# Grouped instance norm on one core: 64 KB rows in every unit but the last six, and the third load moved to ScalarE's queue

## The chip, the cores and the metric

The kernel runs on one core of one Trainium2 chip. The metric is the device time of one execution in microseconds (us), as a median over several runs. Beside the times there is one profiled execution, whose trace gives the start and length of every instruction and of every DMA packet.

## The reference

For each of 4 x 8 x 16 = 512 channels of 256 x 256 float32 values, the mean and the variance over the 65,536 values are taken, and each value is normalised and multiplied by the channel's gamma:

```python
mu = x.mean(axis=(3, 4), keepdims=True)
var = ((x - mu) ** 2).mean(axis=(3, 4), keepdims=True)
x_norm = (x - mu) / np.sqrt(var + 1e-5)
out = x_norm * gamma[None, :, :, None, None]
```

The input is 134.22 MB and so is the output; each must cross between HBM and SBUF once.

## The kernel before

A channel is cut into S = 8 rows of 8,192 values (32 KB), so that 16 channels fill 128 partitions. That is one slot: 128 x 32 KB = 4.19 MB. SBUF holds SLOTS = 6 of them, as three tiles of two slots (`pairs`, `xt` in the profile). The 512 channels are 32 slots' worth of work.

The work goes in units. A narrow unit takes one slot: 16 channels, 32 KB in each partition. A wide unit takes the two slots of a pair: 32 channels, four partitions for each, 64 KB in each partition, loaded by one DMA with 64 KB rows. The first six slots' worth and the last six are narrow units and the twenty between them are ten wide units, 22 units in all (`units`).

The loop over units does the same for each. For each half h of the unit (one for narrow, two for wide) VectorE sums the 128 x 8192 values (L154), ScalarE squares and sums them (L155), and TensorE adds these sums up over the partitions of a channel with a small matrix that also scales and negates them (L161). VectorE then forms the negated variance (L165), ScalarE takes the root (L169), VectorE inverts it and multiplies by gamma (L173, L175). Then for each half VectorE normalises in place (L180) and ScalarE's queue stores the half, with 32 KB rows (L184).

Loads are issued by `load(u, queue)` at L71. The first units, as many as fit into six slots (`first`), are loaded ahead of the loop: before, these are the six narrow ones, of which units 1 and 3 go to ScalarE's DMA queue and the others to SyncE's. Each later unit is loaded by SyncE (`nc.sync`) and stands in `behind[u]`: it is issued after the stores of the unit that frees its slots, and waits for these stores to land. So SyncE's queue (q1 in the profile) carries loads alone, and ScalarE's queue (q10) carries all stores and two early loads. The order in which each engine issues is that of the program text; no scheduler changes it.

ScalarE has one stream for its squares, its roots and its DMA issues: a store at L184 waits in that stream for VectorE's normalisation, and the next unit's squares stand behind it. GpSimd loads gamma and builds the two matrices (one for narrow and one for wide units) at the start.

Of the kernel before, what the change touches and what calls it, by code (L numbers as in the profile page):

```python
# [14 lines left out]
@with_exitstack  # L15
def kernel(
    ctx: ExitStack,
    tc: tile.TileContext,
    x: bass.AP,
    gamma: bass.AP,  # L20
    out: bass.AP,
):
    nc = tc.nc
    B, G, C, H, W = x.shape
    P = nc.NUM_PARTITIONS
    HW = H * W
    n_ch = B * G * C
    GC = G * C
    S = 8
    K = P // S  # L30
    F = HW // S
    SLOTS = 6
    ENDS = 6
    assert HW % S == 0 and GC % (2 * K) == 0 and (n_ch // K - 2 * ENDS) % 2 == 0

    xf = x.rearrange("b g c h w -> (b g c h w)")
    of = out.rearrange("b g c h w -> (b g c h w)")
    gv = gamma.rearrange("g c -> (g c)")

    data = ctx.enter_context(tc.tile_pool(name="data", bufs=1))  # L40
    singles = ctx.enter_context(tc.tile_pool(name="singles", bufs=1))
    psum = ctx.enter_context(tc.tile_pool(name="psum", bufs=4, space=bass.MemoryType.PSUM))
    ctx.enter_context(tc.manual_schedule())

    pairs = [data.tile([P, 2, F], F32, name=f"xt{i}") for i in range(SLOTS // 2)]


    units = []
    at = 0
    slot = 0  # L50
    total = n_ch // K
    while at < total:
        wide = 2 if ENDS <= at < total - ENDS else 1
        units.append((at, wide, slot))
        at += wide
        slot = (slot + wide) % SLOTS
    U = len(units)

    def on_chip(u):
        at, wide, slot = units[u]  # L60
        pair = pairs[slot // 2]
        if wide == 2:
            return pair[:].rearrange("p t f -> p (t f)")
        return pair[:, slot % 2]

    def in_dram(flat, u):
        at, wide, slot = units[u]
        return flat[at * K * HW : (at + wide) * K * HW].rearrange("(p f) -> p f", p=P)

    def load(u, queue):  # L70
        queue.dma_start(out=on_chip(u), in_=in_dram(xf, u))  # L71


    held = [units[u][1] for u in range(U)]
    behind = {u: [] for u in range(U)}
    first = 0
    free = SLOTS
    nxt = 0
    while nxt < U and held[nxt] <= free:
        free -= held[nxt]  # L80
        nxt += 1
    first = nxt
    for u in range(U):
        free += held[u]
        while nxt < U and held[nxt] <= free:
            free -= held[nxt]
            behind[u].append(nxt)
            nxt += 1

    g_row = singles.tile([1, GC], F32, name="g_row")  # L90
    nc.gpsimd.dma_start(out=g_row[:], in_=gv[None, :])  # L91
    for u in range(first):
        load(u, nc.scalar if u in (1, 3) else nc.sync)

    eps_t = singles.tile([P, 1], F32, name="eps_t")
    nc.gpsimd.memset(eps_t[:], 1e-5)  # L96
    one = singles.tile([1, 1], F32, name="one")
    nc.gpsimd.memset(one[:], 1.0)

    root_eps = singles.tile([P, 1], F32, name="root_eps")  # L100
    nc.scalar.activation(out=root_eps[:], in_=eps_t[:], func=ACTF.Sqrt)  # L101


    g_all = singles.tile([1, GC * S], F32, name="g_all")
    navg = {}
    g_cols = {}
    for wide in (1, 2):
        s = S // wide
        k = K * wide
        ng = GC // k  # L110
        m = singles.tile([P, k, s], F32, name=f"navg{wide}")
        nc.gpsimd.memset(m[:], -1.0 / HW)  # L112
        nc.gpsimd.affine_select(  # L113
            out=m[:], in_=m[:], pattern=[[-s, k], [0, s]], compare_op=ALU.is_ge,
            fill=0.0, base=0, channel_multiplier=1,
        )
        nc.gpsimd.affine_select(  # L117
            out=m[:], in_=m[:], pattern=[[s, k], [0, s]], compare_op=ALU.is_ge,
            fill=0.0, base=s - 1, channel_multiplier=-1,
        )  # L120
        navg[wide] = m[:].rearrange("p k s -> p (k s)")
        g_rep = g_all[:, : GC * s].rearrange("o (n k s) -> o n k s", n=ng, k=k)
        g_ps = psum.tile([P, ng], F32, name=f"g_ps{wide}", bufs=1)
        g_col = singles.tile([P, ng], F32, name=f"g_col{wide}")
        nc.vector.tensor_copy(  # L125
            out=g_rep,
            in_=g_row[:].rearrange("o (n k) -> o n k", n=ng).unsqueeze(3).to_broadcast([1, ng, k, s]),
        )
        for n in range(ng):
            nc.tensor.matmul(  # L130
                out=g_ps[:, n : n + 1],
                lhsT=g_rep[:, n].rearrange("o k s -> o (k s)"),
                rhs=one[:],
                start=True, stop=True,
            )
        nc.vector.tensor_copy(out=g_col[:], in_=g_ps[:])  # L136
        g_cols[wide] = g_col

    junk = singles.tile([P, F], U8, name="junk")

    st = singles.tile([P, U, 4], F32, name="st")
    nvar = singles.tile([P, U], F32, name="nvar")
    std = singles.tile([P, U], F32, name="std")
    rstd = singles.tile([P, U], F32, name="rstd")
    scale = singles.tile([P, U], F32, name="scale")

    squares = []
    for u in range(U):
        at, wide, slot = units[u]
        t = on_chip(u)  # L150
        ps = psum.tile([P, 2], F32, name="ps")
        for h in range(wide):
            part = t[:, h * F : (h + 1) * F]
            nc.vector.reduce_sum(out=st[:, u, 2 * h : 2 * h + 1], in_=part, axis=AX.X)  # L154
            square = nc.scalar.activation(  # L155
                out=junk[:], in_=part, func=ACTF.Square, accum_out=st[:, u, 2 * h + 1 : 2 * h + 2],
            )
            if squares and h == 0:
                tc.declare_no_dep(square.ins, squares[-1].ins, reason="junk, nobody reads it")
            squares.append(square)  # L160
            nc.tensor.matmul(  # L161
                out=ps[:], lhsT=navg[wide], rhs=st[:, u, 2 * h : 2 * h + 2],
                start=h == 0, stop=h == wide - 1,
            )
        nc.vector.tensor_scalar(  # L165
            out=nvar[:, u : u + 1], in0=ps[:, 0:1], scalar1=ps[:, 0:1],
            scalar2=ps[:, 1:2], op0=ALU.mult, op1=ALU.add,
        )
        nc.scalar.activation(  # L169
            out=std[:, u : u + 1], in_=nvar[:, u : u + 1], func=ACTF.Sqrt,  # L170
            bias=eps_t[:], scale=-1.0,
        )
        nc.vector.reciprocal(out=rstd[:, u : u + 1], in_=std[:, u : u + 1])  # L173
        g = (at % (GC // K)) // wide
        nc.vector.tensor_mul(  # L175
            out=scale[:, u : u + 1], in0=rstd[:, u : u + 1], in1=g_cols[wide][:, g : g + 1],
        )
        for h in range(wide):
            part = t[:, h * F : (h + 1) * F]
            nc.vector.tensor_scalar(  # L180
                out=part, in0=part, scalar1=ps[:, 0:1], scalar2=scale[:, u : u + 1],
                op0=ALU.add, op1=ALU.mult,
            )
            nc.scalar.dma_start(out=in_dram(of, u)[:, h * F : (h + 1) * F], in_=part)  # L184
        for v in behind[u]:
            load(v, nc.sync)
# [30 lines left out]
```

## Time and profile before

| | |
|---|---|
| median of 3 runs | 629.92 us (628.83 to 630.21) |
| profiled execution, its own time | 628.7 us |
| its span, first to last instruction | 627.0 us |
| DVE (VectorE) busy | 435.9 us, 70% of the span |
| ACT (ScalarE) busy | 235.9 us, 38% |
| PE (TensorE) busy | 23.2 us, 4% |
| DMA traffic | 268.47 MB, mean 428 GB/s |

The median is read against other medians. Durations of single instructions and stretches come from the profiled execution and add up to its span; its own time is 1.7 us more than the span. "DMA share" in the profile is the mean busy share of the core's 16 DMA engines in a stretch, and GB/s what they moved in it. A packet is one contiguous row of a transfer here, 32 KB or 64 KB; its bytes are counted in the stretch in which it starts.

### The profile page before, as it was taken

To read this page: it belongs to the slowest core of one execution; us is meant where nothing else is said; L and a number is where in the kernel's file an instruction comes from. 1 tells how busy PE (TensorE), PEld (TensorE's weight loads), DVE (VectorE), ACT (ScalarE), POOL (GpSimd) and SP (SyncE) were. 2 spreads that over 40 slices of the span, in tenths; PEclk is the share of its full clock that TensorE was granted. 3 is DMA by queue.
4 is the path that set the end of the run, shared out by engine and by line. 5 is a ranking of instruction groups with operands and counts; after the bars stand their busy time and mean duration, and the time that the engine had idled before them with its cause. 6 is when DMAs were issued, how large, how long until landed. Compare 5 with 4: busy or idle time off the path is not lost.

```text
span 627.0 us, 588 instructions
## 1 busy us (share of the span) xinstructions
PE 23.2 (4%) x88; PEld 21.3 (3%) x88; DVE 435.9 (70%) x134; ACT 235.9 (38%) x88; POOL 3.1 (0%) x13
## 2 busy tenths in 40 slices
PE   2100000000000000000000000000000000000000
PEld 2100000000000000000000000000000000000000
DVE  0588999693966929669395793957929998668710
ACT  0444444440806308063170722607126444224400
POOL 1000000000000000000000000000000000000000
DMA  8999999999999999999999999999999999999997
GB/s 372 433 424 431 433 395 445 420 452 418 449 416 433 446 414 433 431 448 422 433 458 418 449 418 424 435 464 406 460 406 435 433 433 435 433 435 435 433 432 341
DMA packets 7811, 268.47 MB, mean 428 GB/s; under 512 B 896, under 2 KB 896, under 8 KB 896
## 3 DMA queue, kind: packets, MB, share of 16 engines
q10 hardware_dynamic: 4896, 142.61, 52.8%
q1 hardware_dynamic: 2880, 125.83, 46.7%
q8 instruction: 1, 0.02, 0.0%
q14 instruction: 2, 0.02, 0.0%
q0 software_dynamic: 32, 0.00, 0.0%
HBM read 134.22 MB, written 134.22 MB: 428 GB/s over the span
## 4 chain that ended last, share of the span: by engine, by line
another core or an unknown queue 40%; DMA 33%; DVE 20%; PE 1%; issue 0%; ACT 0%; SPq 0%
DMA xt<-in_x_dram 18%; DMA out_dram<-xt 15%; DVE st L154 14%; DVE xt L180 6%; PE ps L161 1%; ACT std L169 0%; DVE nvar L165 0%; SPq L71 0%; DVE rstd L173 0%; DVE scale L175 0%
## 5 line engine op out<-in xcount | busy, mean ns | idle before, releaser
L154 DVE TENSOR_REDUCE st<-xt 128x1 f32<-128x8192 f32 x32 | 277.0, 8681 | 120.1 <-DMA xt<-in_x_dram 120.1
L155 ACT ACTIVATE junk<-xt 128x8192 uint8<-128x8192 f32 x32 | 225.0, 7030 | 286.9 <-DMA xt<-in_x_dram 244.3
L180 DVE TENSOR_SCALAR xt<-xt,ps,scale 128x8192 f32<-128x8192 f32 x32 | 144.7, 4549 | 0.8
L161 PE MATMUL ps<-st,navg 128*128 128x2 f32 x64 | 17.8, 348 | 557.2 <-DVE st L154 557.2
L161 PEld LDWEIGHTS ps<-st,navg 128*128 128x128 f32 x64 | 16.0, 311 | 559.1 <-issue 559.1
L169 ACT ACTIVATE std<-nvar,eps_t 128x1 f32<-128x1 f32 x22 | 6.5, 295 | 68.7 <-DVE nvar L165 68.7
L165 DVE TENSOR_SCALAR nvar<-ps 128x1 f32<-128x1 f32 x22 | 6.3, 287 | 16.4 <-PE ps L161 16.4
L173 DVE RECIPROCAL rstd<-std 128x1 f32<-128x1 f32 x22 | 3.6, 164 | 8.0 <-ACT std L169 8.0
L125 DVE COPY g_all<-g_row 1x1024 f32<-1x1024 f32 (+1 forms) x2 | 1.1, 542 | 10.6 <-DMA g_row<-in_gamma_dram 10.6
L155 ACT ACTIVATION_READ_ACCUMULATOR junk<-xt 128x1 f32 x32 | 6.0, 186 | 0.0
L130 PE MATMUL g_ps<-one,g_all 1*128 1x1 f32 x24 | 5.4, 348 | 12.0 <-DVE g_all L125 12.0
L130 PEld LDWEIGHTS g_ps<-one,g_all 1*128 1x128 f32 x24 | 5.3, 324 | 12.1 <-issue 11.4
L136 DVE COPY g_col<-g_ps 128x8 f32<-128x8 f32 (+1 forms) x2 | 0.3, 164 | 5.7 <-PE g_ps L130 5.7
L175 DVE TENSOR_TENSOR scale<-rstd,g_col 128x1 f32<-128x1 f32 x22 | 3.5, 159 | 0.7
L101 ACT ACT_TABLE_LOAD x1 | 1.3, 1283 | 1.7 <-PEq L201 1.7
L113 POOL TENSOR_SCALAR_AFFINE_SELECT navg<-navg 128x128 f32<-128x128 f32 x2 | 0.9, 467 | 0.1
L117 POOL TENSOR_SCALAR_AFFINE_SELECT navg<-navg 128x128 f32<-128x128 f32 x2 | 0.9, 458 | 0.1
L91 POOL DMA_DIRECT2D g_row<-in_gamma_dram x1 | 0.6, 607 | 0.8 <-POOLq L201 0.8
L112 POOL MEMSET navg<- 128x128 f32 x2 | 0.4, 217 | 0.0
L101 ACT ACTIVATE root_eps<-eps_t 128x1 f32<-128x1 f32 x1 | 0.2, 203 | 0.0
L96 POOL MEMSET eps_t<- 128x1 f32 x1 | 0.1, 118 | 0.0
L201 POOL MEMSET const-bfloat16-1.0<- 128x1 bf16 x1 | 0.1, 102 | 0.0
(4 smaller groups left out, 0.4 us busy)
## 6 DMA issues: line engine op xcount, KB each, us to landing
out_dram<-xt ACTq DMA_DIRECT2D x32, 4096.0 KB, 46.3
xt<-in_x_dram SPq DMA_DIRECT2D x10, 4096.0 KB, 28.4
xt<-in_x_dram ACTq DMA_DIRECT2D x2, 4096.0 KB, 31.6
xt<-in_x_dram SPq DMA_DIRECT2D x10, 33.1
g_row<-in_gamma_dram POOLq DMA_DIRECT2D x1, 0.5 KB, 9.3
```

The lines of the kernel that those rows point to most:

```text
L101: nc.scalar.activation(out=root_eps[:], in_=eps_t[:], func=ACTF.Sqrt)
L113: nc.gpsimd.affine_select(out=m[:], in_=m[:], pattern=[[-s, k], [0, s]], compare_op=ALU.is_ge, fill=0.0, base=0, channel_multiplier=1,)
L125: nc.vector.tensor_copy(out=g_rep, in_=g_row[:].rearrange("o (n k) -> o n k", n=ng).unsqueeze(3).to_broadcast([1, ng, k, s]),)
L130: nc.tensor.matmul(out=g_ps[:, n : n + 1], lhsT=g_rep[:, n].rearrange("o k s -> o (k s)"), rhs=one[:], start=True, stop=True,)
L154: nc.vector.reduce_sum(out=st[:, u, 2 * h : 2 * h + 1], in_=part, axis=AX.X)
L155: square = nc.scalar.activation(out=junk[:], in_=part, func=ACTF.Square, accum_out=st[:, u, 2 * h + 1 : 2 * h + 2],)
L161: nc.tensor.matmul(out=ps[:], lhsT=navg[wide], rhs=st[:, u, 2 * h : 2 * h + 2], start=h == 0, stop=h == wide - 1,)
L165: nc.vector.tensor_scalar(out=nvar[:, u : u + 1], in0=ps[:, 0:1], scalar1=ps[:, 0:1], scalar2=ps[:, 1:2], op0=ALU.mult, op1=ALU.add,)
L169: nc.scalar.activation(out=std[:, u : u + 1], in_=nvar[:, u : u + 1], func=ACTF.Sqrt, bias=eps_t[:], scale=-1.0,)
L173: nc.vector.reciprocal(out=rstd[:, u : u + 1], in_=std[:, u : u + 1])
L175: nc.vector.tensor_mul(out=scale[:, u : u + 1], in0=rstd[:, u : u + 1], in1=g_cols[wide][:, g : g + 1],)
L180: nc.vector.tensor_scalar(out=part, in0=part, scalar1=ps[:, 0:1], scalar2=scale[:, u : u + 1], op0=ALU.add, op1=ALU.mult,)
```

## The change

ENDS, which kept the first six and the last six slots' worth narrow, becomes LAST, which keeps only the last six. The units are now 13 wide ones and then six narrow ones, 19 in all. Three wide units fill SBUF at the start. The first two are loaded by SyncE's queue ahead of the loop. The third is issued on ScalarE's queue, inside the loop, after ScalarE's second square, that is after both squares of unit 0 and ahead of unit 0's root and of all stores. The rest is as before.

```diff
-    ENDS = 6
-    assert HW % S == 0 and GC % (2 * K) == 0 and (n_ch // K - 2 * ENDS) % 2 == 0
+    LAST = 6
+    assert HW % S == 0 and GC % (2 * K) == 0 and (n_ch // K - LAST) % 2 == 0
...
-        wide = 2 if ENDS <= at < total - ENDS else 1
+        wide = 2 if at < total - LAST else 1
...
-    for u in range(first):
-        load(u, nc.scalar if u in (1, 3) else nc.sync)
+    for u in range(first - 1):
+        load(u, nc.sync)
...
             squares.append(square)
+            if len(squares) == 2:
+                load(first - 1, nc.scalar)
```

## The prediction

> **What bounds the kernel now.** I read the page first: the span, the line of slices and the two DMA queues.
>
> ```profile
> span 627.0 us, 588 instructions
> DMA  8999999999999999999999999999999999999997
> GB/s 372 433 424 431 433 395 445 420 452 418 449 416 433 446 414 433 431 448 422 433 458 418 449 418 424 435 464 406 460 406 435 433 433 435 433 435 435 433 432 341
> DMA packets 7811, 268.47 MB, mean 428 GB/s; under 512 B 896, under 2 KB 896, under 8 KB 896
> q10 hardware_dynamic: 4896, 142.61, 52.8%
> q1 hardware_dynamic: 2880, 125.83, 46.7%
> ```
>
> The DMA engines are busy in every slice, and the two queues' packets take 52.8 + 46.7 = 99.5% of the span. At 433.5 GB/s, the rate of the quiet slices, 268.47 MB take 619.3 us. So 7.7 us of the span are not plain transfer. The first slice (15.7 us, 372 GB/s) lost 2.2 us, the last (341) lost 3.3, and 2.2 went in between. The views by stage say where. The columns that count are the last two, DMA share and GB/s.
>
> ```profile
> core 0: us, PE busy (x) PEld busy (x) DVE busy (x) ACT busy (x) POOL busy (x), PEclk, DMA share, GB/s
> 2.00:38.00 36.00, 5.96 (x26) 5.76 (x26) 15.43 (x10) 8.62 (x5) 2.18 (x8) 1.00 1.00 430
> 38.00:44.00 6.00, 0.00 (x0) 0.00 (x0) 6.00 (x1) 5.82 (x1) 0.00 (x0) 1.00 0.95 355
> 44.00:83.00 39.00, 1.67 (x6) 1.50 (x6) 35.47 (x16) 16.47 (x10) 0.00 (x0) 1.00 1.00 430
> 83.00:93.00 10.00, 0.56 (x2) 0.50 (x2) 8.82 (x5) 7.38 (x3) 0.00 (x0) 1.00 1.07 403
> 93.00:153.00 60.00, 1.67 (x6) 1.50 (x6) 45.14 (x13) 21.96 (x8) 0.00 (x0) 1.00 1.00 431
> 153.00:500.00 347.00, 10.02 (x36) 9.00 (x36) 247.66 (x64) 135.98 (x46) 0.00 (x0) 1.00 1.00 433
> 500.00:620.00 120.00, 3.35 (x12) 3.01 (x12) 77.35 (x30) 39.38 (x18) 0.00 (x0) 1.00 1.00 433
> ```
>
> From 153 us on nothing is lost. Before that, two short stretches move less than their time allows: 38 to 44 us lacks (433 - 355)/433 x 6 = 1.1 us, 83 to 93 us lacks 0.7, and their neighbours 0.3 each, in all about 2.3 us from 38 to 153 us. The two neighbours are within what the counting of packets by their start can shift. In the second stretch the share is 1.07 while fewer bytes move: packets took longer there, the engines did not stand idle. I call these 2.3 us the opening loss. The timeline of ScalarE's queue and of SyncE's says what begins there:
>
> ```profile
> 0.80 0.89 ACTq L71 DMA_DIRECT2D xt<-in_x_dram  x2
> ...
> 37.78 0.35 ACTq L184 DMA_DIRECT2D out_dram<-xt  x1
> ...
> 81.74 41.26 SPq L71 DMA_DIRECT2D xt<-in_x_dram  x2
> ```
>
> The first store is issued at 37.78 (the first row, of two early loads, gives the price of an issue), and SyncE issues its first load with 64 KB rows, the first one to start beside stores, at 81.74.
>
> Then I read the waits of SyncE's queue, the waits of the engines and the chain that ended last, to see that compute only follows.
>
> ```profile
> SPq L71 <- DMA out_dram<-xt: 545.9, 17, 59.6
> ACT junk L155 <- DMA xt<-in_x_dram: 244.3, 15, 21.3
> DVE st L154 <- DMA xt<-in_x_dram: 120.1, 15, 11.9
> 0.81 21.89 DMA xt<-in_x_dram
> 161.35 0.33 SPq L71
> ...
> 393.86 33.16 DMA xt<-in_x_dram
> ...
> 554.69 28.39 DMA xt<-in_x_dram
> 583.08 0.02 issue
> ```
>
> SyncE waits 545.9 us for stores to land so that it may load, and VectorE and ScalarE wait for loads. From 161.35 to 393.86 us the chain shows six more loads, one each (393.86 - 161.35)/6 = 38.75 us. A wide unit moves 16.78 MB, 8.39 each way, which at 433 GB/s is 38.7 us. The kernel is bound by bytes through the 16 DMA engines, and a schedule can change its time only where a queue runs dry or packets go slower than the usual.
>
> **The change, part by part.**
>
> *Rows of 64 KB in place of 32 KB.* Six narrow loads, 25.17 MB, become three wide ones.
>
> ```profile
> 161.30:393.80 232.50, 6.67 (x24) 6.00 (x24) 161.55 (x43) 87.38 (x31) 0.00 (x0) 1.00 1.00 434
> 496.60:615.00 118.40, 3.35 (x12) 3.01 (x12) 80.75 (x30) 42.78 (x18) 0.00 (x0) 1.00 1.00 434
> 598.20:620.00 21.80, 0.00 (x0) 0.00 (x0) 0.00 (x0) 0.00 (x0) 0.00 (x0) 1.00 1.00 433
> ```
>
> The first row is a stretch in which every load has 64 KB rows, the second one in which loads have 32 KB rows. Both move 434 GB/s. With the rounding, the gain or loss on 25.17 MB (58 us) is at most 0.23%, 0.13 us either way. I take 0.
>
> *Three loads fewer.* The first load took 21.89 us from issue to landing, in which two units of 4.19 MB shared the engines; 8.39 MB at 433 GB/s take 19.4. So 2.5 us are launch and receipt, paid at the start once. For the three loads that go this is hidden as long as another queue has packets, which the share of 1.00 shows. I take 0. The Trainium skill, "DMA: Bandwidth & Descriptors", section "Anatomy of one DMA — SWDGE (gpsimd) path", gives each DMA a fixed cost of about 2.0 us beside its bytes; by that price, were it exposed, three loads fewer would bring an estimated 6 us, and the share of 1.00 speaks against it.
>
> *The first 60 us, where only loads can run.* Before, units 0 and 1 arrive together on two queues at 22.70. After, unit 0 is the same 8.39 MB on one queue, ahead of unit 1 in it, and lands at the same 22.7. Its 38.7 us of loads keep SyncE's queue filled till about 2.5 + 38.7 = 41 us. What follows a wide unit's landing is seen on a wide unit of before that landed at 117.74:
>
> ```profile
> 117.74 7.03 ACT L155 ACTIVATE junk<-xt 128x8192 uint8<-128x8192 f32 x1 [10.30 <-DMA xt<-in_x_dram]
> 117.74 17.28 DVE L154 TENSOR_REDUCE st<-xt 128x1 f32<-128x8192 f32 x2 [5.32 <-DMA xt<-in_x_dram]
> 124.89 7.03 ACT L155 ACTIVATE junk<-xt 128x8192 uint8<-128x8192 f32 x1
> 131.83 0.19 ACT L155 ACTIVATION_READ_ACCUMULATOR junk<-xt 128x1 f32 x1
> 136.81 9.01 DVE L180 TENSOR_SCALAR xt<-xt,ps,scale 128x8192 f32<-128x8192 f32 x2
> 141.39 4.80 ACTq L184 DMA_DIRECT2D out_dram<-xt  x2
> ```
>
> The squares end 14.3 us after landing, so the third load is issued at 37.0. Even if all of the 2.5 us passes before its first byte, it joins at 39.5, some 1.7 us ahead of the point where SyncE's queue would run dry. Cost 0. If that cover is missed by x us, the end comes x us later, since no later stage has slack to give back. ScalarE's root and stores of unit 0 stand behind that issue, which takes 0.45 us (0.89 for the two early ones), and they wait for VectorE anyway: the first store follows 23.65 us after landing (141.39 - 117.74), at 46.4, the second at 50.8.
>
> *Stores behind the third load in one queue.* Those stores are queued behind the load's packets and move from about 2.5 + 58.1 = 60.6 us on, where before the first store was issued at 37.78. It moves bytes in time, but takes none: until 60.6 loads fill the engines. From there unit 0's stores need 19.4 us, to 80. Unit 1's work starts at 50.8 (VectorE is done with unit 0 28.1 us after landing), so its stores come at 74.5 and 79, ahead of 80, and 8.39 MB of them cover the start of load 3, which SyncE issues when unit 0's stores have landed, at about 81. Load 3 with unit 1's stores fills the engines to 80 + 38.7 = 119; unit 2's stores are issued by 51 + 28 + 28 = 107. Load 3, at the 33.16 us of a wide load, lands at 114, and its stores come at 138 and 142, well ahead of 119 + 38.7 = 157.5. That is the steady cycle that before shows from 161 us on. No queue is dry at any of these points.
>
> *The tail* is the same six narrow units. The last load of before landed at 583.08 and 37 us of stores alone followed at 433 GB/s, so compute has slack there. 0.
>
> *The opening loss.* Its first part (38 to 44 us) falls where the first stores join loads, its second (83 to 93) where the first 64 KB load joins stores. After, the first stores follow loads in one queue with nothing beside them, and the first loads to join stores do so at 81. I keep the second part whole. The first part lies between 0 and its 1.1 us; it is nearest to a plain change of direction in one queue, which no row shows alone, and I take about half, a gain of 0.4. In full the loss may vanish (-2.3) or double (+2.3), if 64 KB rows pay the second part's price at both places.
>
> Sum: 627.0 - 0.4 = 626.6 of span, 628.3 for the profiled execution (1.7 around the span). The three runs' median of 629.92 stands 1.2 over the profiled execution's 628.7, so I say 629.5 for a median.
>
> **The rivals.**
>
> *The opening loss goes (faster).* If slow packets come only where two queues switch direction in step, a start with loads alone and then stores alone may spare both parts: 629.9 - 2.3 = 627.6. For it: the loss is seen only at two transitions of the first 93 us, and the change redraws just that stretch. Against it: at 81 us loads still join stores, as at 83. It decides once more than half of the 2.3 us goes.
>
> *A lone load queue is slower (slower).* Till 39 us SyncE's queue now works alone, with 64 KB rows. No row of before has loads from one queue only; loads there always have the other queue beside them. If a lone queue leaves gaps between packets, the 36 us run at, say, the 403 GB/s of the stretch where the first 64 KB loads began: 36 x 30/433 = 2.5 us more, 629.5 + 2.5 = 632.0. It matters by 0.2% from a rate under 418. Against it: stores from a lone queue, from 598.2 to 620 us, move 433 GB/s, and I take that row as the nearest. On this the Trainium skill, "DMA: Bandwidth & Descriptors", section "Issuing engines are not separate DMA queues", says that DMAs run on the same 16 engines whichever engine issues them, by which one queue or two give the same time; no run here shows it for loads.
>
> *Every DMA's fixed cost counts (much faster).* Three loads fewer at 2.5 us each, 7.5 us: 622.4. It would need exposed launches, and the share of 1.00 leaves none. The Trainium skill's fixed cost, named above, is the rule that would ask for it.
>
> **How the numbers follow.** A difference under 0.2% (1.26 us) is about what a measurement of this kernel can tell from none; the three runs themselves spread by 1.4 us. The forecast, everything within 1.26 us of before, has 0.69. The opening loss gone has 0.17, the fixed cost 0.02; the lone queue, with the third load coming too late as its lesser kin, 0.12. That is 0.19 faster, 0.69 same, 0.12 slower. Forecast 629.5. The range takes in the faster rival's 627.6 and, above, half of the lone queue's price, 630.8: 627.5 to 630.8; the forecast's own range is 628.7 to 630.6.
>
> **What would show it.** Right: in the profile after, DMA shares near 1.00 and 430 to 434 GB/s from 2 to 38 us; the third load issued near 37 with no dip at 41; stores alone from 61 to 81; slow stretches of some 2 us together near 61 and 81 to 91; then 38.7 us per wide unit. Wrong: a rate under 418 in the first 38 us, a share under 0.9 at 41 or 80, or a start without either slow stretch and a span under 625.4.

## The result, and the profile after

The changed kernel takes 627.93 us (median of 18 runs, 627.42 to 628.88), the kernel before 629.06 in its 18 runs beside it (628.14 to 630.21). The ratio is 0.9982, 95% interval 0.9974 to 0.9989: about 1.1 us faster, clear of the noise and just short of 0.2%. The forecast was 629.5 in a range of 627.5 to 630.8.

The page of the kernel after shows the same picture as before. The DMA engines are busy in every slice, and the span of the profiled execution, 626.8 us, is only 0.2 under that of before. Both are single executions: before's own 628.7 lies under its median, after's 628.54 over its.

```profile
span 626.8 us, 572 instructions
DMA  9999999999999999999999999999999999999997
GB/s 402 401 468 368 435 464 406 462 408 433 452 435 447 410 431 437 442 418 447 412 435 439 429 447 414 458 410 452 410 433 435 435 433 429 435 433 435 434 435 324
```

The stages of the kernel after, with DMA share and GB/s as the last two columns, show where it differs:

```profile
0.00:38.00 38.00, 5.96 (x26) 5.76 (x26) 16.52 (x6) 15.73 (x6) 3.10 (x13) 1.00 0.97 414
38.00:55.00 17.00, 0.56 (x2) 0.50 (x2) 14.85 (x7) 3.44 (x2) 0.00 (x0) 1.00 1.00 432
55.00:65.00 10.00, 0.56 (x2) 0.50 (x2) 10.00 (x2) 9.97 (x3) 0.00 (x0) 1.00 0.96 367
65.00:83.00 18.00, 0.56 (x2) 0.50 (x2) 16.82 (x7) 4.07 (x4) 0.00 (x0) 1.00 1.01 437
83.00:93.00 10.00, 0.56 (x2) 0.50 (x2) 10.00 (x2) 9.97 (x3) 0.00 (x0) 1.00 0.99 426
93.00:160.00 67.00, 1.67 (x6) 1.50 (x6) 46.52 (x14) 22.33 (x9) 0.00 (x0) 1.00 1.01 437
```

One slow stretch is left, from 55 to 65 us, where loads end and stores begin. From 83 to 93, where the kernel before had 403, this one has 426. Ten microseconds are too short to tell by, since a packet's bytes are counted at its start: profiled again, the changed kernel has 419 there and the kernel before 416. Twenty do tell, and so does the time that the load packets on SyncE's queue took. For the kernel before, then the kernel after (of the queue: packets, MB, and their time as a share of 16 engines from 86 to 90 us):

```profile
83.00:103.00 20.00, 0.56 (x2) 0.50 (x2) 18.82 (x6) 12.48 (x4) 0.00 (x0) 1.00 1.04 419
q1 hardware_dynamic: 16, 1.05, 84.1%
```

```profile
83.00:103.00 20.00, 1.12 (x4) 1.00 (x4) 18.82 (x6) 11.90 (x5) 0.00 (x0) 1.00 1.08 465
q1 hardware_dynamic: 19, 1.25, 72.1%
```

Before, 16 packets took 84.1% of 16 engines' 4 us, 3.4 us each; after, 19 took 2.4 us each, which is what 64 KB take in the later cycles too. Profiled again, the two kernels have 419 and 442 GB/s over the same 20 us; in the experiments whose engines never stand idle it is 408 to 423 with the loss and 444 to 472 without. One wider window sums the opening up. It comes out within 2 GB/s (0.6 us) in repeated executions, so I use it from here on. For the kernel before, then the kernel after:

```profile
38.00:160.00 122.00, 3.90 (x14) 3.51 (x14) 99.64 (x33) 55.85 (x21) 0.00 (x0) 1.00 1.00 424
```

```profile
38.00:160.00 122.00, 3.90 (x14) 3.50 (x14) 98.19 (x28) 49.78 (x17) 0.00 (x0) 1.00 1.00 429
```

Against 433 GB/s, before lacks (433 - 424)/433 x 122 = 2.5 us in this window and after 1.1. The difference of 1.4 us, or 0.8 with the second profile of before (426, further down), is the size of the gain.

The timeline of after shows the new opening, step by step:

```profile
22.81 7.03 ACT L155 ACTIVATE junk<-xt 128x8192 uint8<-128x8192 f32 x1 [20.51 <-DMA xt<-in_x_dram]
29.96 7.03 ACT L155 ACTIVATE junk<-xt 128x8192 uint8<-128x8192 f32 x1
29.97 0.39 ACTq L71 DMA_DIRECT2D xt<-in_x_dram  x1
46.46 4.80 ACTq L186 DMA_DIRECT2D out_dram<-xt  x2
51.86 17.28 DVE L154 TENSOR_REDUCE st<-xt 128x1 f32<-128x8192 f32 x2 [0.97 <-DMA xt<-in_x_dram]
75.51 4.80 ACTq L186 DMA_DIRECT2D out_dram<-xt  x2
82.10 0.33 SPq L71 DMA_DIRECT2D xt<-in_x_dram  x1
115.20 17.28 DVE L154 TENSOR_REDUCE st<-xt 128x1 f32<-128x8192 f32 x2 [7.27 <-DMA xt<-in_x_dram]
```

The third load is issued at 29.97, when the second square starts and not when it ends. It therefore shares the engines with the second load, whose unit VectorE gets at 51.86, after 0.97 us of waiting. SyncE's first load beside stores is issued at 82.10 and lands by 115.20. No slow packets come with it.

### The profile page after: what moved, and what is told of

The parts are those of the page before. It is cut to its first block, busy times and chain, and to the rows that moved or that the text cites. A ratio compares the mean times of both kernels' runs of the same rounds, so it can differ in the third digit from the quotient of the medians.

```text
span 626.8 us, 572 instructions
## 1 busy us (share of the span) xinstructions
PE 23.2 (4%) x88; PEld 21.3 (3%) x88; DVE 433.8 (69%) x125; ACT 235.0 (37%) x85; POOL 3.1 (0%) x13
## 4 chain that ended last, share of the span: by engine, by line
another core or an unknown queue 52%; DMA 27%; DVE 14%; SPq 1%; PE 0%; issue 0%; ACT 0%
DMA out_dram<-xt 14%; DMA xt<-in_x_dram 13%; DVE st L154 10%; DVE xt L182 4%; SPq L71 1%; PE ps L163 0%; ACT std L171 0%; DVE nvar L167 0%; DVE rstd L175 0%; DVE scale L177 0%
## 6 DMA issues: line engine op xcount, KB each, us to landing
out_dram<-xt ACTq DMA_DIRECT2D x32, 4096.0 KB, 46.4
```

## The experiments

Each experiment ran beside the kernel before, and its ratio is against that. The first four ask which part of the change brings the gain: the wide rows or the place of the third load.

**All three opening loads on SyncE's queue** (against the changed kernel):

```diff
-    for u in range(first - 1):
+    for u in range(first):
         load(u, nc.sync)
...
-            if len(squares) == 2:
-                load(first - 1, nc.scalar)
```

> All three opening wide loads on SyncE's queue, ahead of the loop; ScalarE's queue carries stores alone. Theory R (rows: the loss near 85 us comes with the first 64 KB load that starts beside stores, and is gone when wide loads run from the start): as the changed kernel, about 1.1 us faster than before (ratio 0.998), no slow stretch between 80 and 95 us. Theory Q (queue: what pays is that the third load stands ahead of all stores on ScalarE's queue, so that loads and stores hardly mix before 80 us): no gain, ratio 1.000 within 0.001, two slow stretches as before.

627.67 us, ratio 0.998 (0.9972 to 0.9989). The gain is all there without ScalarE's queue, and the window of the opening is as good as the changed kernel's:

```profile
38.00:160.00 122.00, 3.91 (x14) 3.51 (x14) 99.07 (x28) 50.92 (x18) 0.00 (x0) 1.00 1.00 430
```

So the third load on ScalarE's queue is not needed for the gain. Theory Q in its strict form falls.

**The second opening load on ScalarE's queue from the start, the third on SyncE's** (against the last one):

```diff
-        load(u, nc.sync)
+        load(u, nc.scalar if u == 1 else nc.sync)
```

> Wide from the start, the second opening load on ScalarE's queue ahead of the loop, the third on SyncE's: two load queues from the first us on. Theory R: ratio 0.998, the gain does not depend on the queues. Theory Q: ratio 1.000 within 0.001. The rival of the prediction, that a lone load queue is slower, would make this one faster than the changed kernel; I expect no difference between the two over 0.1%.

636.69 us, ratio 1.0124 (1.011 to 1.0138): 7 to 8 us slower than before, which no theory had. Its timeline and windows say why:

```profile
41.99 17.28 DVE L154 TENSOR_REDUCE st<-xt 128x1 f32<-128x8192 f32 x2 [22.04 <-DMA xt<-in_x_dram]
65.64 4.80 ACTq L184 DMA_DIRECT2D out_dram<-xt  x2
86.55 0.33 SPq L71 DMA_DIRECT2D xt<-in_x_dram  x1
...
61.00:66.00 5.00, 0.00 (x0) 0.00 (x0) 4.96 (x3) 0.00 (x0) 0.00 (x0) 1.00 0.00 0
...
85.00:90.00 5.00, 0.56 (x2) 0.50 (x2) 3.82 (x5) 0.29 (x1) 0.00 (x0) 1.00 0.61 210
```

Two wide loads on two queues share the engines, and the first unit can start only at 42 us, when both have landed, instead of one after the other. The first store then comes at 65.64, but the 25.17 MB of loads are done at 61: the engines stand still for 5 us, and again for part of 85 to 90. In the changed kernel the first unit lands at 22.8, since its load is alone in front. That order is what a wide opening needs; one queue or two makes no difference as long as it holds.

**The narrow opening with its last two loads late on ScalarE's queue** (against before):

```diff
-    for u in range(first):
-        load(u, nc.scalar if u in (1, 3) else nc.sync)
+    for u in range(first - 2):
+        load(u, nc.sync)
...
             squares.append(square)
+            if len(squares) == 1:
+                load(first - 2, nc.scalar)
+                load(first - 1, nc.scalar)
```

> The narrow opening of before, but with its last two loads issued on ScalarE's queue after the first square, ahead of all stores, and the four others on SyncE's: the change's queue order without its 64 KB rows. Theory Q: ratio 0.998, the second slow stretch near 85 us gone. Theory R: ratio 1.000 within 0.001, the slow stretch near 85 us still there, since the first 64 KB load still starts beside stores.

628.18 us, ratio 0.9988 (0.9979 to 0.9997): faster, if less surely, and its opening is clean as well, though its first 64 KB load starts beside stores:

```profile
38.00:160.00 122.00, 3.91 (x14) 3.51 (x14) 93.71 (x33) 50.19 (x19) 0.00 (x0) 1.00 1.00 430
```

So theory R falls too: 64 KB rows that start beside stores are not by themselves slow. Either half of the change alone gives a clean opening window.

**Every unit narrow** (against before), run twice:

```diff
-        wide = 2 if ENDS <= at < total - ENDS else 1
+        wide = 1
```

> Every unit narrow, 32 units, so that no load has 64 KB rows; queues as before. Theory R: without a 64 KB load the second slow stretch is gone and the time is 1 to 1.5 us under before (ratio 0.998). Theory Q, and any theory by which the second stretch is just the first load that joins stores: slow stretch still there, ratio 1.000. If 32 KB rows cost anything in the steady cycle, it shows here on 84 MB of loads: over 0.3 us I do not expect.

627.75 us, ratio 0.9973 (0.9965 to 0.9982). The second time, beside the changed kernel on one chip:

> The all-narrow kernel again, beside the changed one on one chip: ratio to before 0.997 to 0.998. It decides whether 64 KB rows are worth anything at all: if wide units bring nothing but another opening, this one is not slower than the changed kernel.

627.73 us, ratio 0.9979 (0.997 to 0.9988). The changed kernel, run again with it:

> The changed kernel again, beside the all-narrow one on one chip: ratio to before 0.998 within 0.001, profile with one slow stretch near 58 us and none near 85.

628.14 us, ratio 0.9984 (0.9976 to 0.9993). The intervals overlap, so which of the two is faster stays open, but wide units are worth nothing that shows. With narrow units SyncE issues a load each time one slot comes free, from 62 us on, so loads never stop in the opening, and there is no second slow stretch:

```profile
38.00:160.00 122.00, 4.47 (x16) 4.02 (x16) 110.01 (x41) 59.72 (x25) 0.00 (x0) 1.00 1.00 430
161.30:393.80 232.50, 6.69 (x24) 6.01 (x24) 166.44 (x61) 89.28 (x37) 0.00 (x0) 1.00 1.00 433
```

**The kernel before, profiled again.**

> The kernel before, unchanged, profiled a second time and timed against itself: ratio 1.000 within 0.001, which shows what the comparison can tell. Theory C (coincidence: the slow stretch from 83 to 93 us comes where ScalarE issues a store within 1 us after SyncE issues a load with 64 KB rows, 82.58 after 81.74): the stretch is there again if these two issues stand as close again. Theory D (draw: the stretch comes in some executions and not in others, whatever the kernel): it may be missing with the same issue times.

629.34 us, ratio 1.0005 (0.9996 to 1.0014). The slow stretch is there again, at the same place, so it is no chance draw of one execution:

```profile
83.00:93.00 10.00, 0.56 (x2) 0.50 (x2) 8.82 (x5) 7.30 (x3) 0.00 (x0) 1.00 1.06 416
38.00:160.00 122.00, 3.90 (x14) 3.50 (x14) 100.24 (x33) 56.53 (x21) 0.00 (x0) 1.00 1.00 426
```

**The narrow opening, all loads on SyncE's queue** (`load(u, nc.sync)` for every opening unit of before).

> The opening of before with narrow units, all six loads on SyncE's queue, ScalarE's queue for stores alone. Theory S (split: two early loads on ScalarE's queue make the slow stretch, since it is the one thing that before has and the changed kernel, the one with all wide loads on SyncE and the narrow one with late loads lack): stretch gone, ratio 0.998. Theory C: stretch gone only if the first 64 KB load's issue and a store's issue come to stand over 1.5 us apart.

630.19 us, ratio 1.0016 (1.0007 to 1.0025): the only narrow opening that is slower than before. Its first store is issued at 30.47, 7 us earlier than in before, and the slow stretch at the first stores comes earlier with it, ahead of 38 us, where before has 413:

```profile
0.00:38.00 38.00, 5.96 (x26) 5.76 (x26) 22.65 (x10) 16.01 (x7) 3.12 (x13) 1.00 0.97 398
38.00:160.00 122.00, 3.91 (x14) 3.51 (x14) 90.61 (x33) 46.94 (x20) 0.00 (x0) 1.00 1.00 428
```

Theory S falls: the two early loads on ScalarE's queue are not the cause, since without them the kernel loses more. Its sign, no slow stretch from 83 to 93, did come (433 GB/s there), but the loss had only spread: near 50, 70 and 90 us the loads stop for 1.1 to 1.5 us, and after each stop load packets are slow for a while, 0.3 to 0.5 us each time.

**Unit 3's store held back** (against before; the squares are extra work on the junk tile):

```diff
+            if u == 3:
+                for _ in range(3):
+                    nc.scalar.activation(out=junk[:], in_=junk[:], func=ACTF.Square)
             nc.scalar.dma_start(out=in_dram(of, u)[:, h * F : (h + 1) * F], in_=part)
```

> The kernel before with three more squares of 7 us on ScalarE, of the junk tile, just ahead of unit 3's store, so that this store is issued near 92 us and not 0.8 us after SyncE's first 64 KB load near 82. Nothing else is moved, and stores queued earlier cover the delay. Theory C: the slow stretch is gone and the time falls by about 1.1 us, ratio 0.998. Theories S and D: no change, ratio 1.000 within 0.001.

629.23 us, ratio 1.0005 (0.9996 to 1.0014). The store moved from 82.58 to 91.51, and the slow stretch stayed, at 410 GB/s.

**Unit 1's second store moved to meet the load** (against the changed kernel):

```diff
+            if u == 1 and h == 1:
+                nc.scalar.activation(out=junk[:], in_=junk[:], func=ACTF.Square)
+                nc.scalar.activation(out=junk[:, :64], in_=junk[:, :64], func=ACTF.Square)
             nc.scalar.dma_start(out=in_dram(of, u)[:, h * F : (h + 1) * F], in_=part)
```

> The changed kernel with one more square of 7 us and a short one on ScalarE between unit 1's two stores, so that the second of these stores is issued near 83 us, some 0.8 us after SyncE's first load that starts beside stores (82.10), as in the kernel before. Theory C: a slow stretch from 83 to 93 us appears and the time rises by about 1.1 us, ratio to before 1.000. Theories S and D: as the changed kernel, ratio 0.998.

628.36 us, ratio 0.9989 (0.998 to 0.9998). The load was issued at 81.94 and the store at 82.88, as meant, and the opening window stayed at 429 GB/s. The ratio lies between the two that the theories asked for, so it is the window that decides: theory C falls from both sides.

**The first two wide loads held back** (against before; the loads leave `behind` and are issued in unit 4):

```diff
+            if u == 4:
+                nc.vector.memset(pairs[0][:, 0, 0:1], 0.0)
+                load(6, nc.sync)
+                load(7, nc.sync)
             square = nc.scalar.activation(
```

> The kernel before with its first two 64 KB loads held back until VectorE's sum in unit 4, about 91 us in place of 82 (a one-column write into the first of the freed slots makes the load wait), so that no load moves for some 15 us where before it was 6. The store queue has work all that time. Theory P (pause: loads that stop for a few us beside stores and start again pay about 1.3 us; after a long pause, or without one, they do not): slow stretch near 85 gone and none near 95, ratio 0.998. Theory H (history: what counts is the mixing of loads and stores from 40 to 80 us, not the pause): a slow stretch where the loads start again, near 95, ratio 1.000 or a little over.

629.1 us, ratio 1.0 (0.9992 to 1.0009). The load was issued at 90.97 instead of 81.74, and the slow stretch went with it (the 452 and the 370 are partly the counting by start; over the 20 us it is 411, where before has 419):

```profile
83.00:93.00 10.00, 0.56 (x2) 0.50 (x2) 8.84 (x6) 7.16 (x3) 0.00 (x0) 1.00 1.05 452
93.00:103.00 10.00, 0.00 (x0) 0.00 (x0) 10.00 (x2) 5.33 (x1) 0.00 (x0) 1.00 1.00 370
```

The stretch belongs to the loads' starting again, not to a time or to a store. A stop of 15 us in place of 6 does not spare it: theory P falls up to that length.

**All narrow, but with a stop in the loads** (against the all-narrow kernel):

```diff
+    behind[0], behind[1] = [], [7, 6]
```

> The all-narrow kernel with loads 6 and 7 exchanged in SyncE's order, so that load 6 is issued behind load 7 near 82 us and no longer at 62: no load moves from about 79 to 85 us, as in the kernel before, but the loads that start then have 32 KB rows. Theory P: a slow stretch of about 1 us appears at 85, ratio 0.999 where the all-narrow kernel had 0.9973. Theory R' (it needs the first 64 KB load as well as the pause): none appears, ratio 0.9973 within 0.001. Theory H: it appears.

628.92 us, ratio 0.9997 (0.9988 to 1.0006): the gain of the all-narrow kernel is gone. The load that it issued at 62 is issued behind another at 82, and slow stretches appear with 32 KB rows alone:

```profile
83.00:93.00 10.00, 0.56 (x2) 0.50 (x2) 8.82 (x5) 7.28 (x3) 0.00 (x0) 1.00 1.03 423
93.00:103.00 10.00, 0.00 (x0) 0.00 (x0) 10.00 (x2) 5.21 (x1) 0.00 (x0) 1.00 0.99 393
38.00:160.00 122.00, 3.91 (x14) 3.51 (x14) 98.36 (x36) 53.85 (x22) 0.00 (x0) 1.00 1.00 424
```

Rows of 64 KB are not needed for the loss, and in this pair the stop is: without it the window has 430, with it 424. This is one edit, made and undone, that turns the loss on and off. It also exchanges two loads and issues both within 2 us, which no run separates from the stop.

## Why the prediction was right, and where it was not

The bound was read rightly. DMA bytes set the time in all kernels but the one whose engines stood idle, the steady cycle after is (430.96 - 120.77)/8 = 38.77 us for a wide unit against 38.75 before, and the last 460 us move 433 GB/s here, 434 and 433 in the two profiles of before, where one step of the rounding is 1.1 us:

```profile
120.77 0.33 SPq L71
...
430.96 32.67 DMA xt<-in_x_dram
...
160.00:620.00 460.00, 13.38 (x48) 12.01 (x48) 319.14 (x93) 169.51 (x63) 0.00 (x0) 1.00 1.00 433
```

*Rows of 64 KB at 0, three loads fewer at 0.* Right: all-narrow kernels, with 13 loads more than the changed one, are no slower. The much faster rival, every DMA's fixed cost, fell by that.

*The first 60 us.* The unit landed at 22.8 and the first store was issued at 46.46, as worked out (22.7 and 46.4). The third load's issue was 7 us earlier than worked out, 29.97 and not 37.0, because a DMA issue on ScalarE's queue goes when the square ahead of it has started. That widened the cover that I had put at 1.7 us. The lone load queue was not slower: up to 38 us after moved 414 GB/s, on one queue until the third load is issued at 29.97, before 413 on two. With all three opening loads on SyncE's queue it is 414 as well. That rival fell. The sign that I had named, 430 to 434 GB/s from 2 to 38 us, did not come (422), but by the counting alone: this kernel has 262 GB/s from 0 to 2 us, and from 0 on the two are alike.

*Stores behind the third load.* Right: stores alone from about 61 to 82, load 3 issued at 82.10 (81 expected) and landed by 115.20 (114 expected), with no dry queue. The experiment in which two wide loads land together shows what late stores cost: the engines stood idle 5 us in one stretch.

*The opening loss* is the step that was wrong in size, and by its parts. I put its first part at 1.1 us and took half of it away, and its second at 0.7 and kept it whole, a gain of 0.4 us. It was the other way round. The first part stayed (the changed kernel has its one slow stretch from 55 to 65 us, and the window from 38 to 160 still lacks 1.1 us), and the second went altogether. The sizes were wrong too, because the windows count a packet's bytes at its start. Spread over the time that each packet took, the bytes in the same two traces make the first part 0.8 us before and 1.1 after, and the second 1.4 us before and nothing after; the losses of 0.3 that I saw in the neighbours belong to these two. So 0.3 us were lost and 1.4 gained, together the measured 1.1. The second profiles have 0.8 and 1.0 for before, 1.2 and nothing for after.

The outcome lies between the forecast and the rival in which the opening loss goes, for which I had asked that more than half of the 2.3 us go: by the time 1.1 us went, by the window 1.4 of 2.5, so it stands on the border of the two. The forecast's own range, 628.7 to 630.6, missed the median of 627.93, which lies inside 627.5 to 630.8 only because I had stretched the range to take in that rival. Part of the miss is the reference: the three runs that I had gave 629.92 for before, 18 runs give 629.06. The upper ends did not fit my own words either: 1.26 us over 629.92 is 631.2.

My reason for keeping the second part, that at 81 us loads still join stores, names a condition that is not enough. In after, in the kernel with all wide loads on SyncE, and in the narrow one with late loads, loads start again beside stores near 82 to 86 and lose nothing. What the runs show is this: the loss goes with loads that start again after a stop (it moved with them, and came and went with the stop), and it needs something else that the three clean openings lack. What that is stays open. The length of the rows, a store issued close by, and early loads on ScalarE's queue were each tried and are not it. The length of the stop is not settled: no load packet moves for 6 us in before and for 15 where the loads were held back, both with the loss, but for 19, 19 and 23 us in the three clean openings. Length alone cannot be all, since stops of 10 to 11 us between the later loads of before cost nothing, and stops of 1.1 to 1.5 us in the narrow kernel with all loads on SyncE cost something. That the clean ones let their first store move later fits them too: its first packet starts at 61.5 us in after, 51.7 and 56.3 in the other two (in the last it is issued at 30.18, but behind two loads in its queue), against 43.1 in before and 34.6 in the narrow kernel with its first store issued at 30.47, which loses most. A late first store and a long stop come together in all of these, and neither was tried alone.

## What to carry to other kernels

When the DMA engines are busy from end to end, look for slow packets, not for idle engines: a window whose share is 1.0 but whose GB/s are low is where time can still be had, and a few us around the first stores may be all of it. Compare openings by one wide window that starts and ends in steady traffic, over repeated executions; it told openings apart here at the size of 1 us in 628, where single spans did not. It misses what falls outside: the narrow opening with all loads on one queue has 428 in it, against 424 before, and is the slower kernel, because its slow stretches begin ahead of 38 us. And with wide units, let the first unit's load run alone in front: two loads on two queues share the engines, and the first store, the first free slot and the next load all wait for both (8.4 MB each here, 7 to 8 us). With narrow units this did not pay: the opening with all six loads on one queue was the slowest of the narrow ones, and the all-narrow kernel, whose first two loads share the engines, was not slower than any.

## What the hardware showed that was not expected

Loads that start again beside stores early in the run can have slow packets at first: in before a load packet of 64 KB took 3.4 us from 86 to 90 us, where it takes 2.4 later. All 16 engines are busy meanwhile (a DMA share of 1.02 to 1.04 over 83 to 103 us, at 419 GB/s in two executions of before), and it costs 1.0 to 1.5 us in all. Later starts in the same kernels, once in every 38.7 us cycle, show nothing of this size (433 GB/s from 153 to 500 us). And a DMA issue that stands behind a 7.03 us square in ScalarE's stream is not held by it: it was issued at 29.97, 0.01 us after that square began at 29.96.
